# Last pair's new sample state among its value projections, one norm chain for prompt and sample, and a shared tile for accumulators and gates

## The chip, the cores and the metric

The kernel runs on one core of one Trainium2 chip. The metric is the device time of one execution in microseconds, the median of several runs; lower is better. A profiled execution gives the trace that is quoted here. Its engines are TensorE (PE, with PEld for the weight loads), VectorE (DVE), ScalarE (ACT), GpSimd (POOL) and SyncE (SP), which issues most DMAs.

## The reference

One step of a hybrid decoder layer, for a prompt of 1024 tokens and a sample of 8 sequences with 4 new tokens each (32 rows). An RMSNorm feeds one input projection. Head group A is sparse attention: an indexer scores the keys, the top 256 are chosen, and 8 query heads attend to them, with a position bias. For the sample the keys lie in a paged cache of 8192 positions. Head group B is retention with 8 heads of 64. Both branches are gated, concatenated and projected, then comes a post-norm, the residual and a gated embedding. What matters here is group B:

```python
def step(S, inp):                       # chunks of 128 tokens
    inter = einsum('bchk,bhkv->bchv', qc * dec_in, S)
    scores = einsum('bchk,bshk->bhcs', qc, kc) * dmat
    intra = einsum('bhcs,bshv->bchv', scores, vc)
    S = S * dec_chunk + einsum('bchk,bchv->bhkv', kc * dec_out, vc)
    return S, inter + intra
...
yb = silu(gb) * _head_norm(ob)          # mean and variance of each head's 64 values
```

It is done for the prompt (state from zero, eight chunks) and for the sample (state given for each sequence, one chunk of 4). The final states of both are outputs.

## The kernel before, in words

The program is written in one order, and a scheduler decides the order in which each engine gets it, from a model of the times; the engines then run their own queues in that order and wait on semaphores. The buffers of a pool are reused tile by tile: who takes a buffer over waits for the last use of the old tile, its DMAs included.

After the indexer and the prompt's selection, retention runs over four pairs of heads (hp = 0 to 3; here pair 0 to pair 3). Each pair has two stages on TensorE:

- the query/key stage: eight blocks of 128 tokens, 24 matmuls each (L276 to L278, tile pqk; three products of split fp32 values), and eight matmuls for the sample (L285). Each block is rotated on VectorE (L1047 to L1049) and GpSimd (L1051, L1052).
- the value stage: the same for values and gates (tile pvg). take_vg copies each block's values (L1060, vv) and takes silu of its gates (L1062, sg) on ScalarE. Then come the chunk's matmuls: two transposes (L1068, L1069), scores (L1078), masked on VectorE (L1079, sm), the state's update (L1489, added up in sbd at L1494) and the outputs (L1498, L1500), which ScalarE copies into the accumulator (L1502, acc, one tile of 9 blocks, the ninth for the sample).

After block 7 the sample's turn (ret_sample, from L1129): its old states are loaded (s0), its values and gates taken (vvs, sgs), its outputs computed (L1139, L1141) and added up (L1143 to L1145), and its new state is made: a masked copy of the values for each head (vm, L1150), one matmul for each (dst, L1152), added to the old state (sso, L1156, L1157) and written out (L1158).

Then norm_gate, twice. For the prompt, 16 columns (8 blocks by 2 heads): statistics (L1088, L1089), variance plus epsilon (gv, L1094), square root on ScalarE and reciprocal (gy, L1097, L1098), one Newton step (gz, L1104 to L1106, L1112, L1113), the scaling of each column (three of four on ScalarE, L1117; the fourth on VectorE, L1119), the multiplication with the gates (L1122; on GpSimd, and on VectorE for pair 3), and one DMA to a buffer in DRAM (yb_d, L1123). For the sample the same with two columns of 32 rows.

Beside these run pieces of two generators: the bisection that finds the sample's 256th score (during pairs 0 and 1, at high priority, L872 to L1017, with a conditional part behind a branch at L976 through which all engines go), and the sample's selection (from pair 1 on, L1203 to L1282, with L1234, and gathers of key and value rows, L1170). Matmuls of both stand between those of the pairs.

PSUM banks: three for pqk and pvg (tag b), three for ret and dst (tag c). acc has one buffer; sg has ten, vv three. All these tiles are in the pool rt on the right side of SBUF. When retention ends, rt is closed, and attention's tiles take the same addresses: the first score tiles (L) lay over norm_gate's temporaries and over acc, vv, sg, qkT and sm.

Attention begins with the bias tiles (near, L1583, from a DMA of toep, L1551), the scores on TensorE (sa, L1596, L1597), the score with bias and maximum on VectorE (L1602), the exponential on ScalarE (L1605).

Of the kernel before, what the change touches and what calls it, by code (L numbers as in the profile page):

```python
# [10 lines left out]
F32 = mybir.dt.float32  # L11
# [4 lines left out]
AF = mybir.ActivationFunctionType  # L16
# [6 lines left out]
NS = 32  # L23
# [97 lines left out]
def tile_step(ctx: ExitStack, tc: tile.TileContext, I, O):  # L121
# [911 lines left out]
    s0 = rt.tile([128, 8, 128], F32, name="s0")  # L1033
    for t in (*sbd, s0):
        nc.gpsimd.memset(t, 0.0)
# [19 lines left out]
    def take_vg(src, rows, tb, hp, name):  # L1055

        vv = rt.tile([128, 2, 64], F32, tag="vv", bufs=3, name=f"vv{name}")
        sg = rt.tile([128, 128], F32, tag="sg", bufs=10, name=f"sg{name}")
        for j in range(2):
            nc.scalar.activation(vv[:rows, j, :], src[:rows, j * 64:j * 64 + 64], AF.Copy,  # L1060
                                 scale=vsc[:rows, tb, 2 * hp + j:2 * hp + j + 1])
        nc.scalar.activation(sg[:rows], src[:rows, 128:256], AF.Silu)  # L1062
        return vv.rearrange("p h v -> p (h v)"), sg
# [18 lines left out]
    def norm_gate(acc, sgs, ntb, rows, tb0, hp):  # L1082

        nh = ntb * 2
        st = rt.tile([128, 16, 6], F32, tag="st", bufs=2, name="bst")
        mv = rt.tile([128, 16, 2], F32, tag="mv", bufs=2, name="bmv")
        for i in range(nh):
            nc.vector.bn_stats(st[:rows, i, :], acc[:rows, i // 2, (i % 2) * 64:(i % 2) * 64 + 64])  # L1088
            nc.vector.bn_aggr(mv[:rows, i, :], st[:rows, i, :])  # L1089
        v = rt.tile([128, 16], F32, tag="gv", bufs=1, name="gv")  # L1090
        y = rt.tile([128, 16], F32, tag="gy", bufs=1, name="gy")
        z = rt.tile([128, 16], F32, tag="gz", bufs=1, name="gz")
        v_, y_, z_ = v[:rows, :nh], y[:rows, :nh], z[:rows, :nh]
        nc.vector.tensor_tensor(v_.rearrange("p (t h) -> p t h", h=2),  # L1094
                                mv[:rows, :nh, 1].rearrange("p (t h) -> p t h", h=2),
                                epsn[:rows, tb0:tb0 + ntb, 2 * hp:2 * hp + 2], op=ALU.add)
        nc.scalar.activation(y_, v_, AF.Sqrt)  # L1097
        nc.vector.reciprocal(y_, y_)  # L1098
        one = [slice(i, i + 1) for i in range(nh)]
        if nh == 2:  # L1100
            for i in one:
                nc.vector.tensor_scalar(z_[:, i], y_[:, i], y_[:, i], v_[:, i], op0=ALU.mult, op1=ALU.mult)
        else:
            nc.vector.tensor_tensor(z_, y_, y_, op=ALU.mult)  # L1104
            nc.vector.tensor_tensor(z_, z_, v_, op=ALU.mult)
        nc.vector.tensor_scalar(z_, z_, -0.5, 1.5, op0=ALU.mult, op1=ALU.add)  # L1106
        if nh == 2:
            for n, i in enumerate(one):
                nc.vector.tensor_scalar(y_[:, i], y_[:, i], z_[:, i], None, op0=ALU.mult)
                nc.vector.tensor_scalar(z_[:, i], mv[:rows, n, 0:1], y_[:, i], -1.0, op0=ALU.mult, op1=ALU.mult)  # L1110
        else:
            nc.vector.tensor_tensor(y_, y_, z_, op=ALU.mult)  # L1112
            nc.vector.scalar_tensor_tensor(z_, mv[:rows, :nh, 0], -1.0, y_, op0=ALU.mult, op1=ALU.mult)  # L1113
        for i in range(nh):
            a = acc[:rows, i // 2, (i % 2) * 64:(i % 2) * 64 + 64]
            if i % 4 < 3:
                nc.scalar.activation(a, a, AF.Identity, bias=z_[:, i:i + 1], scale=y_[:, i:i + 1])  # L1117
            else:
                nc.vector.tensor_scalar(a, a, mv[:rows, i, 0:1], y_[:, i:i + 1],  # L1119
                                        op0=ALU.subtract, op1=ALU.mult)  # L1120
        for t in range(ntb):
            (nc.vector if hp == 3 else nc.gpsimd).tensor_tensor(acc[:rows, t, :], acc[:rows, t, :], sgs[t][:rows], op=ALU.mult)  # L1122
        nc.sync.dma_start(yb_d[:rows, tb0:tb0 + ntb, hp, :], acc[:rows, :ntb, :])  # L1123
# [5 lines left out]
    def ret_sample(hp, qk, sh, acc):  # L1129
# [3 lines left out]
        vv, sg = take_vg(sh, NS, 8, hp, f"s{hp}")  # L1133
        r, qkT, sm = chunk_mm(qk, vv, 8, NS, smask, hp)
        qm = rt.tile([128, 8, NS], F32, tag="vm", bufs=1, name="qm")
# [8 lines left out]
        for j in (0, 2, 3):  # L1144
            nc.vector.tensor_tensor(acc[:NS, 8, :], r[NS * j:NS * j + NS, 0:128], acc[:NS, 8, :], op=ALU.add)  # L1145
        d = bank("dst", "c")
# [13 lines left out]
        return sg  # L1160
# [289 lines left out]
    for hp in range(4):  # L1450
# [22 lines left out]
        acc = rt.tile([128, 9, 128], F32, tag="acc", bufs=1, name=f"acc{hp}")  # L1473
        sgs = []
# [3 lines left out]
        for tb in range(8):  # L1478
# [5 lines left out]
            vv, sg = take_vg(pt, 128, tb, hp, f"{hp}_{tb}")  # L1484
            sgs.append(sg)
# [16 lines left out]
            nc.scalar.copy(acc[:, tb, :], o)  # L1502
            if tb == 7:
                sgS = ret_sample(hp, qks[8], sh, acc)
        steps(hp)
        so = rt.tile([128, 64], F32, tag="so", bufs=2, name=f"so{hp}")
# [4 lines left out]
        norm_gate(acc, sgs, 8, 128, 0, hp)  # L1511
        norm_gate(acc[:, 8:9, :], [sgS], 1, NS, 8, hp)
# [335 lines left out]
```

## Time and profile before

| | us |
|---|---|
| median of 3 runs (lowest, highest) | 1051.2 (1048.44, 1052.79) |
| profiled execution, its own time | 1050.72 |
| its span | 1048.9 |
| TensorE busy | 991.8 |
| pair 1's value stage begins | 432.3 |
| pair 2 begins | 470.0 |
| pair 3 begins | 503.8 + 40.6 = 544.4 |
| pair 3's value projections end | 623.0 |
| first attention score on VectorE | 647.2 |

The mean granted clock of TensorE is 0.976 of full speed. The page of the profile gives busy time by engine and the chain of work that ended last; views of the trace give stretches by stage (windows), waits by engine, groups of instructions by line, and the instructions one by one (timeline). In rows "out<-in" names the tiles, "<-DVE mn" what ended a wait.

### The profile page before, as it was taken

The numbers are of one execution on the slowest core, as the hardware profiler recorded it, in microseconds if no ns is written. First come the engines' busy times: TensorE is split into PE (matmuls) and PEld (weight loads), VectorE is DVE, ScalarE is ACT, GpSimd is POOL, SyncE is SP. The second block draws the span as 40 slices with busy tenths as digits, with TensorE's granted clock in tenths as the row PEclk, the third lists the DMA queues.
The fourth block names the chain that finished last, engine by engine and source line by source line (L and its number), as shares of the span: only waits on it lengthen the run. The fifth ranks groups of instructions, "written<-read, shape, count | busy, mean of one in ns | idle before, by whom it ended". The sixth has DMA issues, their size and how long they took to land.

```text
span 1048.9 us, 19845 instructions
## 1 busy us (share of the span) xinstructions
PE 991.8 (95%) x7375; PEld 838.2 (80%) x7375; DVE 681.4 (65%) x2022; ACT 503.1 (48%) x1090; POOL 320.8 (31%) x425
## 2 busy tenths in 40 slices
PE   4999998999999899999899995999999999999998
PEld 3999997766776898889788783666666999999998
DVE  6847668898492657969949937787763423873332
ACT  5545565885434487612342335656545523442211
POOL 4203223121301522705803512634330522332200
PEclk9999999999999999999899995999999999999999
DMA  8211235545443311311210724533211312432211
GB/s 291 71 61 51 96 97 190 186 148 177 130 161 115 76 33 43 81 45 47 64 54 21 190 65 128 162 78 109 73 56 48 118 42 81 148 116 87 83 41 38
DMA packets 98310, 102.25 MB, mean 97 GB/s; under 512 B 21346, under 2 KB 88386, under 8 KB 95906
## 3 DMA queue, kind: packets, MB, share of 16 engines
q1 hardware_dynamic: 92450, 74.74, 23.7%
q0 software_dynamic: 5760, 26.22, 8.0%
q8 instruction: 58, 0.95, 0.4%
q14 instruction: 42, 0.34, 0.1%
HBM read 79.25 MB, written 21.68 MB: 96 GB/s over the span
## 4 chain that ended last, share of the span: by engine, by line
PE 45%; DVE 6%; DMA 2%; issue 1%; POOL 1%; ACT 1%; SPq 0%; DVEq 0%; ACTq 0%; POOLq 0%
PE ob L1620 4%; PE ptp L1612 4%; PE pg L276 3%; PE pg L278 3%; PE pg L277 3%; PE po L276 3%; PE po L277 3%; PE po L278 2%; PE sa L1596 2%; PE pvg L276 2%; PE pvg L277 2%; PE pvg L278 2%; PE sa L1597 1%; PE pty L1667 1%; PE pqk L276 1%
## 5 line engine op out<-in xcount | busy, mean ns | idle before, releaser
L1170 POOL DMA_INDIRECT kvs<-in_cache_kv,idx x64 | 64.2, 1003 | 84.1 <-ACT pT L1617 49.1
L276 PE MATMUL pvg<-whi_vgb,xh 128*128 128x256 f32 x256 | 76.2, 298 | 3.0 <-ACT sg L1062 1.8
L276 PE MATMUL pqk<-whi_qkb,xh 128*128 128x256 f32 x256 | 75.0, 293 | 3.3 <-DVE rp L1049 3.3
L277 PE MATMUL pvg<-wlo_vgb,xh 128*128 128x256 f32 x256 | 75.6, 295 | 0.0
L278 PE MATMUL pvg<-whi_vgb,xl 128*128 128x256 f32 x256 | 75.1, 293 | 0.0
L277 PE MATMUL pqk<-wlo_qkb,xh 128*128 128x256 f32 x256 | 74.1, 290 | 0.0
L276 PE MATMUL po<-whi_o,yTh 128*128 128x256 f32 x256 | 73.1, 286 | 0.4 <-DVE yaT L1631 0.4
L278 PE MATMUL pqk<-whi_qkb,xl 128*128 128x256 f32 x256 | 73.2, 286 | 0.0
L278 PE MATMUL po<-whi_o,yTl 128*128 128x256 f32 x256 | 72.8, 285 | 0.0
L276 PE MATMUL pg<-whi_g,yTh 128*128 128x256 f32 x256 | 72.7, 284 | 0.0
L277 PE MATMUL po<-wlo_o,yTh 128*128 128x256 f32 x256 | 72.7, 284 | 0.0
L278 PE MATMUL pg<-whi_g,yTl 128*128 128x256 f32 x256 | 72.3, 283 | 0.0
L277 PE MATMUL pg<-wlo_g,yTh 128*128 128x256 f32 x256 | 72.2, 282 | 0.0
L1605 ACT ACTIVATE L<-L,mn 128x128 f32<-128x128 f32 (+7 forms) x64 | 49.6, 777 | 15.0 <-DVE mn L1602 14.6
L511 DVE SCALAR_TENSOR_TENSOR score<-r,wi,score 128x384 f32<-128x384 f32 (+5 forms) x42 | 41.0, 976 | 23.0 <-ACT r L507 21.7
L1805 DVE TENSOR_TENSOR sgm<-pu,sgm 128x256 f32<-128x256 f32 x32 | 13.6, 424 | 64.8 <-PE pu L278 61.1
L276 PEld LDWEIGHTS pvg<-whi_vgb,xh 128*128 128x128 f32 x256 | 49.8, 195 | 5.4 <-ACT sg L1062 2.2
L276 PEld LDWEIGHTS pqk<-whi_qkb,xh 128*128 128x128 f32 x256 | 49.0, 191 | 6.4 <-issue 5.5
L186 POOL TENSOR_TENSOR wlo_g<-wraw_g,whi_g 128x256 fp32r<-128x256 f32 x32 | 27.1, 881 | 87.8 <-ACT whi_g L185 87.7
L1051 POOL TENSOR_TENSOR qk<-rp,rp 128x128 f32<-128x128 f32 (+1 forms) x36 | 29.6, 821 | 78.7 <-DVE rp L1048 49.3
L507 ACT ACTIVATE r<-si 128x384 f32<-128x384 f32 (+5 forms) x48 | 36.3, 758 | 32.0 <-PE si L365 30.6
L278 PEld LDWEIGHTS pqk<-whi_qkb,xl 128*128 128x128 f32 x256 | 49.1, 192 | 2.4 <-issue 2.4
(545 smaller groups left out, 3317.9 us busy)
## 6 DMA issues: line engine op xcount, KB each, us to landing
wraw_qkb<-in_w_in SPq DMA_DIRECT2D x16, 256.0 KB, 4.1
wraw_vgb<-in_w_in SPq DMA_DIRECT2D x16, 256.0 KB, 3.8
wraw_o<-in_w_out SPq DMA_DIRECT2D x8, 512.0 KB, 5.6
qas<-qas_d SPq DMA_DIRECT2D x8, 512.0 KB, 5.1
xr<-in_x_prompt SPq DMA_DIRECT2D x8, 512.0 KB, 3.9
wraw_g<-in_w_ple_gate SPq DMA_DIRECT2D x8, 512.0 KB, 4.3
out_y_prompt<-sgm SPq DMA_DIRECT2D x32, 128.0 KB, 1.7
qas_d<-qst SPq DMA_DIRECT2D x8, 384.0 KB, 2.7
```

The costliest lines, as they stand in the source:

```text
L186: nc.gpsimd.tensor_tensor(lo[:, k, :n], raw, hi[:, k, :n].bitcast(F32), op=ALU.subtract)
L276: nc.tensor.matmul(pt[:, :n], ah, hi[:, k, :n], start=(k == 0), stop=False)
L277: nc.tensor.matmul(pt[:, :n], ah, lo[:, k, :n], start=False, stop=False)
L278: nc.tensor.matmul(pt[:, :n], al, hi[:, k, :n], start=False, stop=(k == kc - 1))
L507: nc.scalar.activation(r[:, :n], s[:, :n], AF.Relu)
L511: nc.vector.scalar_tensor_tensor(sc, r[:, :n], wi[:, qb, h:h + 1], sc, op0=ALU.mult, op1=ALU.add)
L1051: nc.gpsimd.tensor_tensor(q4[:, :, 0, :], t1[:rows, :, 0, :], t2[:rows, :, 0, :], op=ALU.subtract)
L1170: return nc.gpsimd.indirect_dma_start(out=dst, out_offset=None, in_=kvflat, in_offset=bass.IndirectOffsetOnAxis(ap=idx, axis=0))
L1596: nc.tensor.matmul(s[:, :wc], qas[:, h, :], kah[kv][:, c:c + wc], start=True, stop=False)
L1605: behind[0] = nc.scalar.activation(L[:, :n], L[:, :n], AF.Exp, bias=least, scale=-1.0, accum_out=sm[:, i4:i4 + 1])
L1612: nc.tensor.transpose(tp[:, i4 * 128:i4 * 128 + 128], P[i4][:, kb * 128:kb * 128 + 128], ident)
L1620: nc.tensor.matmul(ob[64 * o:64 * o + 64, :256], vtok[:, kb, kv * 64:kv * 64 + 64], pT[:, o * 256:o * 256 + 256], start=(kb == 0), stop=(k ...
```

## The change

Five things, in one diff:

- A tile ag of 9 blocks by 2 by 128 values holds accumulators (index 0) and gates (index 1). It replaces acc (one buffer) and sg (ten buffers), and has one buffer.
- norm_gate treats prompt and sample in one chain of 18 columns; the rows of the sample's two columns above 32 hold 1.0. The tiles gv, gy, gz, mv and st have one buffer. Two DMAs write yb_d, one for the prompt, one for the sample.
- ret_sample is split: sample_in (old states, values and gates), ret_sample (outputs) and new_state (vm, dst, sso). For pair 3, sample_in and new_state stand after block 3; for the others new_state stands after norm_gate.
- The sample's values have a tile of their own (vvs).
- The tiles of eight tags, ag and the norm's among them, are allocated first in rt, at the low addresses (120672 to 133344). The first score tiles of attention (151264 to 167648) no longer lie over them; the second and third group's key/value tiles (115936 to 134368) now do.

The lines move: before's L1062, L1117, L1502, L1152, L1596, L1602 are L1070, L1115, L1504, L1157, L1603, L1609 after it.

```diff
+    first = {t: rt.tile(shape, F32, name=t, tag=t, bufs=n) for t, shape, n in (
+        ("vm", [128, 8, NS], 1), ("mv", [128, 18, 2], 1), ("gv", [128, 18], 1), ("gy", [128, 18], 1),
+        ("gz", [128, 18], 1), ("st", [128, 18, 6], 1), ("ag", [128, 9, 2, 128], 1), ("so", [128, 64], 2))}
+
+    def rtile(shape, tag, n, name):
+        if tag in first:
+            return first.pop(tag)
+        return rt.tile(shape, F32, tag=tag, bufs=n, name=name)
...
-    def take_vg(src, rows, tb, hp, name):
-
-        vv = rt.tile([128, 2, 64], F32, tag="vv", bufs=3, name=f"vv{name}")
-        sg = rt.tile([128, 128], F32, tag="sg", bufs=10, name=f"sg{name}")
+    def take_vg(src, rows, tb, hp, name, sg, tag="vv"):
+
+        vv = rt.tile([128, 2, 64], F32, tag=tag, bufs=3 if tag == "vv" else 1, name=f"vv{name}")
...
+    mv = first.pop("mv")
+    nc.gpsimd.memset(mv[:, 16:, :], 1.0)
...
+    def norm_gate(ag, hp):
+
+        acc = ag[:, :, 0, :]
+        st = rtile([128, 18, 6], "st", 1, "bst")
+        rows = [128] * 16 + [NS] * 2
+        for i, n in enumerate(rows):
+            nc.vector.bn_stats(st[:n, i, :], acc[:n, i // 2, (i % 2) * 64:(i % 2) * 64 + 64])
+            nc.vector.bn_aggr(mv[:n, i, :], st[:n, i, :])
+        v, y, z = (rtile([128, 18], t, 1, t) for t in ("gv", "gy", "gz"))
+        nc.vector.tensor_tensor(v.rearrange("p (t h) -> p t h", h=2),
+                                mv[:, :, 1].rearrange("p (t h) -> p t h", h=2),
+                                epsn[:, :, 2 * hp:2 * hp + 2], op=ALU.add)
+        nc.scalar.activation(y, v, AF.Sqrt)
+        nc.vector.reciprocal(y, y)
+        nc.vector.tensor_tensor(z, y, y, op=ALU.mult)
+        nc.vector.tensor_tensor(z, z, v, op=ALU.mult)
+        nc.vector.tensor_scalar(z, z, -0.5, 1.5, op0=ALU.mult, op1=ALU.add)
+        nc.vector.tensor_tensor(y, y, z, op=ALU.mult)
+        nc.vector.scalar_tensor_tensor(z, mv[:, :, 0], -1.0, y, op0=ALU.mult, op1=ALU.mult)
+        for i, n in enumerate(rows):
+            a = acc[:n, i // 2, (i % 2) * 64:(i % 2) * 64 + 64]
             if i % 4 < 3:
-                nc.scalar.activation(a, a, AF.Identity, bias=z_[:, i:i + 1], scale=y_[:, i:i + 1])
+                nc.scalar.activation(a, a, AF.Identity, bias=z[:n, i:i + 1], scale=y[:n, i:i + 1])
             else:
-                nc.vector.tensor_scalar(a, a, mv[:rows, i, 0:1], y_[:, i:i + 1],
-                                        op0=ALU.subtract, op1=ALU.mult)
-        for t in range(ntb):
-            (nc.vector if hp == 3 else nc.gpsimd).tensor_tensor(acc[:rows, t, :], acc[:rows, t, :], sgs[t][:rows], op=ALU.mult)
-        nc.sync.dma_start(yb_d[:rows, tb0:tb0 + ntb, hp, :], acc[:rows, :ntb, :])
+                nc.vector.tensor_scalar(a, a, mv[:n, i, 0:1], y[:n, i:i + 1], op0=ALU.subtract, op1=ALU.mult)
+        for t in range(9):
+            n = rows[2 * t]
+            (nc.vector if hp == 3 else nc.gpsimd).tensor_tensor(acc[:n, t, :], acc[:n, t, :], ag[:n, t, 1, :], op=ALU.mult)
+        nc.sync.dma_start(yb_d[:, :8, hp, :], acc[:, :8, :])
+        nc.sync.dma_start(yb_d[:NS, 8, hp, :], acc[:NS, 8, :])
...
-    def ret_sample(hp, qk, sh, acc):
+    def sample_in(hp, sh, ag):
         for j in range(2):
             js = slice(j * 64, j * 64 + 64)
             nc.sync.dma_start(s0[js, :, js], I["state_ret"][0, :, 2 * hp + j].rearrange("b d v -> d b v"))
-        vv, sg = take_vg(sh, NS, 8, hp, f"s{hp}")
+        return take_vg(sh, NS, 8, hp, f"s{hp}", ag[:, 8, 1, :], "vvs")
+
+    def ret_sample(hp, qk, vv, ag):
+        acc = ag[:, :, 0, :]
         r, qkT, sm = chunk_mm(qk, vv, 8, NS, smask, hp)
-        qm = rt.tile([128, 8, NS], F32, tag="vm", bufs=1, name="qm")
+        qm = rtile([128, 8, NS], "vm", 1, "qm")
...
+    def new_state(hp, qk, vv):
...
-        acc = rt.tile([128, 9, 128], F32, tag="acc", bufs=1, name=f"acc{hp}")
-        sgs = []
+        ag = rtile([128, 9, 2, 128], "ag", 1, f"ag{hp}")
...
-            vv, sg = take_vg(pt, 128, tb, hp, f"{hp}_{tb}")
-            sgs.append(sg)
+            vv = take_vg(pt, 128, tb, hp, f"{hp}_{tb}", ag[:, tb, 1, :])
...
-            nc.scalar.copy(acc[:, tb, :], o)
+            nc.scalar.copy(ag[:, tb, 0, :], o)
+            if tb == (3 if hp == 3 else 7):
+                vvs = sample_in(hp, sh, ag)
+                if hp == 3:
+                    new_state(hp, qks[8], vvs)
             if tb == 7:
-                sgS = ret_sample(hp, qks[8], sh, acc)
+                ret_sample(hp, qks[8], vvs, ag)
...
-        norm_gate(acc, sgs, 8, 128, 0, hp)
-        norm_gate(acc[:, 8:9, :], [sgS], 1, NS, 8, hp)
+        norm_gate(ag, hp)
+        if hp < 3:
+            new_state(hp, qks[8], vvs)
```

More of the change, by code (lines that the diff above doesn't have):

```diff
@@ L1062, in take_vg @@
         nc.scalar.activation(sg[:rows], src[:rows, 128:256], AF.Silu)
-        return vv.rearrange("p h v -> p (h v)"), sg
+        return vv.rearrange("p h v -> p (h v)")
     def chunk_mm(qk, vv, tb, rows, mask_ap, hp):
@@ L1080, in chunk_mm @@
         return r, qkT, sm
[L1082 to L1115, printed above, removed]
@@ L1159, in ret_sample @@
             O["ret_state_sample"][0, :, 2 * hp:2 * hp + 2].rearrange("b h d v -> (h d) b v"), so)
-        return sg
     sel_d = dram.tile([2, NS * 64], BF16, name="sel_d")
@@ L1501, in tile_step @@
                                  start=(tb == 0 and j == 0), stop=(j == 1))
-            nc.scalar.copy(acc[:, tb, :], o)
+            nc.scalar.copy(ag[:, tb, 0, :], o)
[3 more added lines that the diff above has]
+                    new_state(hp, qks[8], vvs)
             if tb == 7:
-                sgS = ret_sample(hp, qks[8], sh, acc)
+                ret_sample(hp, qks[8], vvs, ag)
         steps(hp)
-        so = rt.tile([128, 64], F32, tag="so", bufs=2, name=f"so{hp}")
+        so = rtile([128, 64], "so", 2, f"so{hp}")
         for j in range(2):
```

## The prediction

> **What bounds the kernel now.** I read the page first: the totals, then the chain that ended last.
>
> ```profile
> span 1048.9 us, 19845 instructions
> PE 991.8 (95%) x7375; PEld 838.2 (80%) x7375; DVE 681.4 (65%) x2022; ACT 503.1 (48%) x1090; POOL 320.8 (31%) x425
> PE 45%; DVE 6%; DMA 2%; issue 1%; POOL 1%; ACT 1%; SPq 0%; DVEq 0%; ACTq 0%; POOLq 0%
> ```
>
> TensorE is busy for 991.8 of 1048.9 us. Time can come only from the 57 us in which it idles, from stretches at a low granted clock, or from matmuls moved. So I next asked for busy time by stage. The rows are: pair 1's value and gate projections, pair 2's query/key stage, its value stage, the same two of pair 3, and the passage into attention. Columns: busy time and count for PE, PEld, DVE, ACT, POOL, then clock, DMA share and GB/s.
>
> ```profile
> 432.30:470.00 37.70, 35.22 (x290) 32.05 (x288) 27.84 (x92) 11.81 (x37) 14.09 (x26) 1.00 0.27 68
> 470.00:503.80 33.80, 33.80 (x284) 29.69 (x284) 30.76 (x81) 7.41 (x19) 19.84 (x20) 1.00 0.19 58
> 503.80:544.40 40.60, 36.63 (x275) 33.31 (x275) 28.15 (x83) 19.64 (x52) 17.95 (x25) 0.92 0.22 55
> 544.40:584.20 39.80, 39.10 (x342) 33.35 (x341) 35.63 (x138) 9.12 (x27) 13.21 (x22) 1.00 0.15 42
> 584.20:623.00 38.80, 37.11 (x309) 34.34 (x308) 23.68 (x102) 14.45 (x49) 12.16 (x21) 0.96 0.48 123
> 623.00:647.20 24.20, 12.22 (x76) 6.97 (x74) 15.80 (x69) 12.02 (x33) 5.70 (x8) 0.65 0.54 160
> ```
>
> The passage (last row) is the worst stretch: 12 of 24.2 us idle, at a clock of 0.65. The four rows before it hold 0 + 3.97 + 0.70 + 1.69 = 6.4 us of idle time. Their clock costs (1 - 0.92) x 36.6 = 2.9 and (1 - 0.96) x 37.1 = 1.5 us more. The waits of TensorE name the two largest single causes: first for 470 to 623, then for the passage.
>
> ```profile
> PE pfx L1234 <- DVE sm L1232: 2.6, 1, 2.6
> ...
> PE sa L1596 <- DVE mn L1602: 8.1, 1, 8.1
> ```
>
> The first is a step of the sample's top-k selection, late on VectorE. The second is the first attention score, late because VectorE is still normalising pair 3. The timeline of the passage, in order of start (start, duration):
>
> ```profile
> 630.18 1.62 DVE L1583 TENSOR_TENSOR near<-toep,cst 128x512 f32<-128x512 f32 x2 [0.71 <-DMA toep<-toep_d]
> 632.28 0.35 DVE L1088 BATCH_NORM_STATS2 bst<-acc 128x6 f32<-128x64 f32 x2
> 633.27 1.97 PE L1152 MATMUL dst<-vm,qk 32*64 32x512 f32 x2 [1.99 <-DVE vm L1150]
> 633.81 0.15 DVE L1094 TENSOR_TENSOR gv<-bmv,cst 128x16 f32<-128x16 f32 x1
> 638.00 1.41 DVE L1156 TENSOR_TENSOR sso<-dst,s 64x512 f32<-64x512 f32 x2 [1.63 <-PE dst L1152]
> 639.44 0.17 DVE L1106 TENSOR_SCALAR gz<-gz 128x16 f32<-128x16 f32 x1
> 640.39 4.09 ACT L1117 ACTIVATE acc<-acc,gz,gy 128x64 f32<-128x64 f32 x12 [6.18 <-DVE gz L1113]
> 646.89 0.28 DVE L1122 TENSOR_TENSOR acc<-acc,sgs 32x128 f32<-32x128 f32 x1 [0.72 <-ACT acc L1117]
> 647.20 0.29 DVE L1602 CUSTOM_DVE_ANT_0 L<-sa,near 128x128 f32<-128x128 f32 x1
> ...
> 647.41 0.28 DVE L1602 CUSTOM_DVE_ANT_0 L<-sa,near 128x128 f32<-128x128 f32 x1
> ```
>
> VectorE is in program order: L1106 stands behind L1156, which waits for the half-speed dst matmuls. Then come the identities, the gates, and a whole second chain for the sample, up to 647.20.
>
> **Part 1, the passage: a gain of 6.1 us, of which 2.1 are paid elsewhere.** On TensorE, before, after the sample's last retention matmuls (L1139, L1141; dst is the new state, sa the first scores):
>
> ```order
> L1139 MATMUL ret_7771<-s0_3680,qm_7781 32x128 x8
> L1141 MATMUL ret_7771<-vvs3_7766,sm_7776 32x64 x2
> L1152 MATMUL dst_7797<-vm_7798,qk3_8_7368 64x512
> L1152 MATMUL dst_7797<-vm_7801,qk3_8_7368 64x512
> L1596 MATMUL sa_7962<-kahi_7908,qas0_7942 128x128
> L1597 MATMUL sa_7962<-kalo_7909,qas0_7942 128x128
> ```
>
> And now, at the same place:
>
> ```order
> L1500 MATMUL ret_7684<-sbd1_3679,qkT_7687 128x128
> L1502 MATMUL ret_7684<-vv3_7_7680,sm_7689 128x64 x2
> L1141 MATMUL ret_7701<-s0_3680,qm_7711 32x128 x8
> L1143 MATMUL ret_7701<-vvs3_7501,sm_7706 32x64 x2
> L1603 MATMUL sa_7864<-kahi_7810,qas0_7844 128x128
> L1604 MATMUL sa_7864<-kalo_7811,qas0_7844 128x128
> ```
>
> The dst matmuls are gone from here; they now stand among pair 3's value projections. In VectorE's program the first score still stands behind the whole norm, its eight gates and the sample's gate. So the passage gets shorter, but it does not vanish. With T for the end of the value projections (623.0): the bias tiles (near) end at 631.8, so T+8.8, set by a DMA that is not touched. From the first stats behind them (632.28) to gv (633.81) before took 1.5 us with a 0.7 us tile of the new state in between; with the sample's two columns and three adds put in, I take 2.1: T+10.9. Square root, reciprocal and five short steps at 0.17 each, with two handovers between engines: about 2.1, T+13.0. Fourteen identities at 4.09/12 = 0.34: 4.8, T+17.8. The last gates: 0.3, T+18.1. Before it was 647.2 - 623.0 = 24.2. The gain is 6.1 us. The moved dst matmuls cost their time in the stream; all sixteen, by line:
>
> ```profile
> L1152 PE MATMUL dst<-vm,qk x16: 587/638/1112, 423.5 to 636.9; 32*64 32x512 f32 x16
> ```
>
> Four a pair, at 587 to 638 ns: 2.1 us overlapped. Net -4.1. Bounds: -6.5, if they hide in gaps, to -2, if the clock or the bias DMA is later. The wait for the first score stays some 8 us long, so the low clock there stays too.
>
> **Part 2, a new wait between pairs 0 and 1: +16 us.** Gates and accumulators now share one tile (ag), of which there is one. Before, the gate of pair 1's first block (L1062) had a buffer of its own. Now its silu must wait until pair 0's ag has been normalised, gated and written out by both DMAs. ScalarE before (pair 1's blocks; sg1_0 is the first gate):
>
> ```order
> L1117 ACTIVATE acc0_4193<-acc0_4193,gz_4961,gy_4960 128x64 x12
> L1097 ACTIVATE gy_5002<-gv_5001 32x2
> L185 CAST whi_qkb2_5461<-wraw_qkb20_5463 128x1024
> L1060 ACTIVATE vv1_0_5517<-pvg_5471,cst_63 128x64 x2
> L1062 ACT_TABLE_LOAD
> L1062 ACTIVATE sg1_0_5518<-pvg_5471 128x128
> ```
>
> Now (ag_3687 is pair 0's tile, ag1_5423 pair 1's):
>
> ```order
> L976 UNCONDITIONAL_BRANCH
> L1068 ACTIVATE vv1_2_5631<-pvg_5584,cst_63 128x64 x2
> L1115 ACTIVATE ag_3687<-ag_3687,gz_3685,gy_3684 128x64 x12
> L1115 ACTIVATE ag_3687<-ag_3687,gz_3685,gy_3684 32x64 x2
> L1070 ACT_TABLE_LOAD
> L1070 ACTIVATE ag1_5423<-pvg_5448 128x128
> ```
>
> Pair 0's identities have moved behind the third block's values and behind the branch (L976). On VectorE, the rows around that branch are now:
>
> ```order
> L976 UNCONDITIONAL_BRANCH x2
> L992 SCALAR_TENSOR_TENSOR ssm_3791<-ssm_3791 128x1
> L1109 TENSOR_SCALAR gz_3685<-gz_3685 128x18
> L994 CAST sbits_3787<-ssm_3791 128x1
> L1087 TENSOR_TENSOR sm_5640<-ret_5635,cst_63 128x128
> L1110 TENSOR_TENSOR gy_3684<-gy_3684,gz_3685 128x18
> L996 TENSOR_TENSOR sbits_3787<-sbits_3787 128x1
> L1496 TENSOR_TENSOR sbd0_3678<-ret_5566,sbd1_3679 64x64 x2
> L1111 SCALAR_TENSOR_TENSOR gz_3685<-mv_3682,gy_3684 128x18
> L872 TENSOR_SCALAR sjk_3780,ssm_3791<-Xt_3778,sbits_3787 128x2080
> L1117 TENSOR_SCALAR ag_3687<-ag_3687,mv_3682,gy_3684 128x64 x4
> ```
>
> Pair 0's norm is split: its end has slid past the branch of the bisection and past L872. The times of these in the trace of before: the gates' group on GpSimd and its sample gate, the write's landing (pair 0's, then all pairs'), the first gate, the fourth block's first matmul, the first accumulator copy, the end of the branch, L872 and the wait on it.
>
> ```profile
> L1122 POOL TENSOR_TENSOR acc<-acc,sg 128x128 f32<-128x128 f32 x8 | 5.5, 713 | 0.0
> L1122 POOL TENSOR_TENSOR acc<-acc,sgs 32x128 f32<-32x128 f32 x1 | 1.4, 1431 | 0.0
> ...
> DMA to landing us min/median/max: 4.5/4.5/4.5
> ...
> DMA to landing us min/median/max: 1.4/3.1/9.2
> ...
> 440.63 0.28 ACT L1062 ACTIVATE sg<-pvg 128x128 f32<-128x128 f32 x1
> ...
> 445.95 0.37 PE L276 MATMUL pvg<-whi_vgb,xh 128*128 128x256 f32 x1
> ...
> 450.19 0.27 ACT L1502 COPY acc<-ret 128x128 f32<-128x128 f32 x1 [4.34 <-PE ret L1500]
> ...
> 452.96 0.22 DVE L992 SCALAR_TENSOR_TENSOR ssm<-ssm 128x1 f32<-128x1 f32 x1 [3.13 <-DVEq L976]
> 453.60 2.38 DVE L872 TENSOR_SCALAR_CACHE_REDUCE sjk<-Xt,sbits 128x2080 bf16<-128x2080 f32 x1
> ...
> 456.04 0.38 PE L874 MATMUL stot<-ssm,groupr 128*128 128x1 f32 x2 [1.49 <-DVE sjk L872]
> ```
>
> The branch ends at 452.96 as before (bounds 451.5 and 455.5: the same bisection stands ahead of it, between other steps). L1111 follows 1.8 us later, at 454.8. Fourteen identities take it to 459.6; VectorE's four columns come after L872, at about 458.3. GpSimd's nine gates at 0.5 to 0.7, the last longer, end at about 462 (460 to 465). The write took 4.5 here and 3.1 in the median of all; I take 3: 465. The silu, held with its table load, adds about 1, and the fourth block, whose projection needs the PSUM bank, starts at 466 instead of 445.95. By then TensorE has done about 6.4 us of what stood behind 445.95 before (the chunk matmuls of three blocks, the small ones of the bisection, the 1.49 us wait). Of the 470.0 - 445.95 = 24 us to pair 2, 17.7 remain: 483.7. A clock loss comes on top; rows around two earlier gaps:
>
> ```profile
> 592.00:597.00 5.00, 4.68 (x25) 4.55 (x26) 4.91 (x24) 2.53 (x6) 2.91 (x7) 0.66 0.99 264
> ...
> 517.00:525.00 8.00, 5.98 (x27) 5.54 (x28) 7.78 (x30) 4.67 (x16) 5.47 (x11) 0.57 0.01 2
> ```
>
> They lost 0.34 x 5 = 1.7 and 0.43 x 8 = 3.4 us of clock; I take 2.3, so pair 2 begins at 486, +16. Bounds: with the early values of each step +11, with the late ones +21.
>
> Two rules of the Trainium skill speak here. "TensorE: Matmul & The Clock Gate", section on why this matters for your kernels, warns of idle gaps of TensorE over about 3 us, and Part 1 puts the return to full speed at about 3.4 us of sustained work: a loss of 1.7 us. The first row agrees, the second is double; by the rule the sum would be 0.6 us less. "SBUF — State Buffer", section on the DMA setup-cost knee, gives 2 us plus bytes over 436 GB/s: an estimate of 3.2 us for the 512 KB write. The measured 4.5 is longer; by the row the sum would be 1.3 us more.
>
> **Part 3, what is paid back: -10.** While TensorE stands still, VectorE and GpSimd go on with the selection, so pairs 2 and 3 find it further ahead. At most the 6.4 + 2.9 + 1.5 = 10.8 us of the four rows above go; I take 10 (bounds 4 and 10.8, since waits on rope and on pair 2's own state are not selection).
>
> **Part 4, new cost in pairs 2 and 3: +3.** In VectorE's program the selection groups (L1271, L1277, L1282) move from pair 3's query/key stage into pair 2's value stage, where VectorE now also has all of pair 1's leftovers.
>
> ```profile
> L1271 DVE TENSOR_SCALAR oh<-slot,sm 128x256 bf16<-128x256 bf16 x32 | 13.3, 445 | 2.0 <-PE psl L1273 2.0
> L1277 DVE TENSOR_TENSOR le<-psl,cst 128x384 bf16<-128x384 f32 (+1 forms) x11 | 5.9, 537 | 0.1
> L1282 DVE TENSOR_REDUCE row<-le 128x6 f32<-128x384 bf16 (+1 forms) x11 | 5.8, 525 | 0.0
> ```
>
> Together 25 us, most of which ran in the row from 544.4 (VectorE busy for 35.6). Pair 2's value stage has 40.6 us, of which VectorE filled 28.2; with over half of these groups added it is near full, so I take single waits of 3 us; bounds 0 and 7. The same shared tile makes pair 2's and 3's first gates wait for the write too, but the norm runs early there and the blocks' banks cover most of it.
>
> **The sum.** -4.1 + 16 - 10 + 3 = +4.9 on the profiled execution of 1050.7 us (span 1048.9 and 1.8 around it), which lies 0.5 us under the median of 1051.2: 1050.7 + 4.9 is 1055.6, I say 1055.5. The rest is taken to be the same: fewer short steps on VectorE, and the new addresses of the score tiles, cost or give nothing I can find, since before, the second score (647.41) follows the first (647.20) without a wait.
>
> **The rivals.** *A. The stall is short (faster).* If pair 0's norm runs ahead of the branch in fact, or the gates and the write are quick (write 1.4, as its shortest in other pairs), the fourth block starts near 457 and the stall is +7. Paid back in full, with 1 of new cost: -4.1 + 7 - 10.8 + 1 = -7: 1044. Against it: the order of VectorE is fixed, and the norm's end stands behind the branch. *B. Little is paid back (slower).* If VectorE stays the late one in pairs 2 and 3 with the moved groups, -4.1 + 16 - 4 + 6 = +14: 1065. It decides if VectorE's busy time in pair 2's value stage passes about 95%. For it: 35.6 of 39.8 us in pair 3's query/key stage already. *C. No effect.* A stall at its low end, 12, against full payback: -4.1 + 12 - 10.8 + 3 = 0: 1051. *D. Part 1 does nothing*, because the first score waits for the bias or for key tiles: +4 on the forecast, 1059.5; it lies in the range.
>
> **How the numbers follow.** The bound for a difference is 0.5%, about 5.3 us, what a measurement of this kernel can tell from no change: under 1046 is faster, over 1056.5 slower. The forecast case with its own spread (1049 to 1062, D in it) has 0.55: 0.25 of it no change and 0.30 slower, as 1055.5 lies near the edge. A has 0.22 (faster), B 0.10 (slower), C 0.13 (no change). That gives 0.22, 0.38 and 0.40. The range of eight in ten reaches from A's value to B's: 1044 to 1065.
>
> **What would show it.** In the profile after: TensorE idle by 12 to 18 us in pair 1's value stage, ended by ScalarE's L1070, which waits for the write of ag; query/key of pair 2 some 16 us later; the wait on L1234 gone; the passage 18 us instead of 24, with no dst in it. The forecast is wrong if that idle time is under 8 us, or if pair 3's value projections end less than 3 or more than 16 us later than at 623.0.

## The result, and the profile after

The changed kernel takes 1060.2 us (median of 6 runs, 1057.24 to 1062.48) against 1050.1 (6 runs, 1048.44 to 1052.79): a ratio of 1.0088, 95% interval 1.0061 to 1.0115. It is slower by 0.9%. The forecast was 1055.5, with 0.40 on slower and a range of 1044 to 1065: right in its direction and its range, 4.7 us too low.

The profiled execution took 1060.73 us. The page of the profile, totals and chain, as shown of before:

```profile
span 1059.0 us, 19805 instructions
PE 990.1 (93%) x7375; PEld 841.2 (79%) x7375; DVE 669.5 (63%) x1986; ACT 499.9 (47%) x1084; POOL 313.5 (30%) x426
PE 48%; DVE 4%; DMA 2%; ACT 2%; issue 1%; POOL 0%; another core or an unknown queue 0%; SPq 0%; ACTq 0%; DVEq 0%; POOLq 0%
```

The same 7375 matmuls, and VectorE, ScalarE and GpSimd a little less busy. TensorE is busy for 1.7 us less, so the 10 us are idle time: 68.9 us instead of 57.1. The stages, in the order of the table of before (pair 1's value stage, pair 2, pair 2's value stage, pair 3, its value stage, the passage):

```profile
433.00:483.20 50.20, 41.02 (x289) 36.46 (x288) 36.74 (x112) 17.97 (x54) 14.75 (x26) 0.83 0.25 68
483.20:518.70 35.50, 35.37 (x294) 30.48 (x294) 34.12 (x100) 11.19 (x28) 17.03 (x24) 1.00 0.14 35
518.70:560.90 42.20, 38.88 (x331) 36.17 (x330) 23.07 (x102) 14.96 (x48) 13.68 (x23) 0.92 0.22 60
560.90:594.80 33.90, 33.90 (x297) 29.83 (x297) 28.95 (x116) 11.04 (x28) 19.23 (x34) 1.00 0.28 77
594.80:631.10 36.30, 36.30 (x295) 32.21 (x294) 14.60 (x58) 10.76 (x38) 3.22 (x7) 1.00 0.41 102
631.10:649.70 18.60, 7.71 (x70) 6.12 (x68) 12.45 (x55) 11.47 (x30) 5.70 (x8) 0.70 0.59 172
```

Pair 2 begins 13.2 us later than before (483.2 against 470.0). The value projections of pair 3 end only 8.1 later, so 5.1 are won back on the way. The passage shrinks from 24.2 to 18.6 us, and the first score stands at 649.7, 2.5 later than before. Up to here the sum is what was forecast, and better by 2.4 us. The rest comes behind the first score, in a stage that the diff doesn't touch. Attention, from the first score to the output projection, cut into 13, 20, 20, the middle and the last 20 us. Before:

```profile
647.20:660.20 13.00, 12.32 (x66) 9.39 (x67) 9.36 (x37) 8.23 (x28) 7.62 (x7) 0.60 0.40 116
660.20:680.20 20.00, 18.46 (x137) 11.49 (x135) 15.41 (x64) 13.40 (x39) 12.08 (x13) 1.00 0.64 192
680.20:700.20 20.00, 20.00 (x156) 12.87 (x155) 15.77 (x59) 11.52 (x28) 8.74 (x8) 1.00 0.36 93
700.20:793.20 93.00, 93.00 (x692) 59.13 (x691) 66.85 (x239) 55.03 (x109) 34.95 (x37) 1.00 0.26 74
793.20:813.20 20.00, 19.59 (x181) 12.24 (x178) 6.06 (x17) 8.24 (x18) 0.54 (x2) 1.00 0.11 37
```

After:

```profile
649.70:662.70 13.00, 12.58 (x69) 9.42 (x69) 9.88 (x41) 8.33 (x29) 7.49 (x7) 0.64 0.50 142
662.70:682.70 20.00, 15.74 (x111) 9.92 (x111) 12.40 (x51) 11.19 (x33) 10.28 (x12) 0.91 0.52 154
682.70:702.70 20.00, 19.41 (x136) 11.28 (x132) 15.10 (x59) 10.71 (x27) 9.74 (x9) 1.00 0.41 122
702.70:803.70 101.00, 101.00 (x748) 64.57 (x745) 70.09 (x249) 57.64 (x117) 38.59 (x39) 1.00 0.26 76
803.70:823.70 20.00, 17.79 (x169) 11.26 (x166) 5.48 (x15) 7.64 (x16) 0.00 (x0) 1.00 0.04 13
```

The stretch is 166.0 us before and 174.0 after, for the same 1222 matmuls (one that spans a cut is counted in two rows). Idle time is 2.6 before and 7.5 after. Three places stand out: the second row (4.26 idle, clock 0.91), the third (0.59), and the last (2.21 against 0.41).

Why should attention change at all? The order of each engine's queue is set by the scheduler's model of the times, and in attention it differs. Counted in the two traces, from the first score to the output projection, 682 of TensorE's 1222 matmuls stand at another place of its queue, the first of them 11 us behind the first score, and 181 of VectorE's 412 instructions. The last products of the sample show it best. In the changed kernel the sample's last sums (oS) come behind the prompt's last (ob), before they did not; the first and the last start stand behind the durations in each row. The rows by tile, ob and oS, of before:

```profile
L1620 PE MATMUL ob<-pT,vtok x288: 378/380/689, 653.6 to 812.2; 128*64 128x256 f32 x144
...
L1397 PE MATMUL oS<-kvs,PT x128: 272/273/297, 691.8 to 811.7; 128*32 128x128 f32 x128
```

And of after:

```profile
L1627 PE MATMUL ob<-pT,vtok x288: 379/379/690, 655.5 to 818.0; 128*64 128x256 f32 x144
...
L1401 PE MATMUL oS<-kvs,PT x128: 272/273/297, 701.3 to 822.4; 128*32 128x128 f32 x128
```

So at the end there is nothing left to fill the sample's last chain with, and TensorE waits for VectorE's copy of the weights for the sample's new tokens (PN), a wait that before does not have:

```profile
PE oS L1396 <- DVE PN L1393: 1.5, 1, 1.5
```

### The profile page after: what moved, and what is told of

It is laid out like the page before. It is cut to its first block, busy times and chain, and to the rows that moved or that the text cites. A ratio compares the mean times of both kernels' runs of the same rounds, so it can differ in the third digit from the quotient of the medians.

```text
span 1059.0 us, 19805 instructions
## 1 busy us (share of the span) xinstructions
PE 990.1 (93%) x7375; PEld 841.2 (79%) x7375; DVE 669.5 (63%) x1986; ACT 499.9 (47%) x1084; POOL 313.5 (30%) x426
## 4 chain that ended last, share of the span: by engine, by line
PE 48%; DVE 4%; DMA 2%; ACT 2%; issue 1%; POOL 0%; another core or an unknown queue 0%; SPq 0%; ACTq 0%; DVEq 0%; POOLq 0%
PE ob L1627 4%; PE ptp L1619 4%; PE pg L276 3%; PE pg L278 3%; PE pg L277 3%; PE po L276 3%; PE po L277 3%; PE po L278 3%; PE pvg L276 2%; PE sa L1603 2%; PE pvg L277 2%; PE pvg L278 2%; PE sa L1604 2%; PE pqk L278 1%; PE pqk L276 1%; PE pqk L277 1%
## 5 line engine op out<-in xcount | busy, mean ns | idle before, releaser
L1603 PE MATMUL sa<-kahi,qas 128*128 128x512 f32 (+3 forms) x96 | 41.1, 430 | 12.3 <-DVE mn L1609 12.3
L277 PEld LDWEIGHTS pvg<-wlo_vgb,xh 128*128 128x128 f32 x256 | 50.6, 198 | 1.3 <-issue 0.8
```

Source lines behind the costliest of these rows:

```text
L277: nc.tensor.matmul(pt[:, :n], ah, lo[:, k, :n], start=False, stop=False)
L1603: nc.tensor.matmul(s[:, :wc], qas[:, h, :], kah[kv][:, c:c + wc], start=True, stop=False)
```

## The experiments

Two theories for the 8 us behind the first score: the **order** (the scheduler's new order of attention costs them, whatever brought it about) and the **addresses** (later key and value tiles now lie over the tiles allocated first, and attention waits for them). For retention: the **write** (pair 1's gates wait for the shared tile to be written out) and the **place** (the norm's end behind the branch is enough). All ratios are to the kernel before on the same chip.

### Gates in buffers of their own

```diff
-        ("gz", [128, 18], 1), ("st", [128, 18, 6], 1), ("ag", [128, 9, 2, 128], 1), ("so", [128, 64], 2))}
+        ("gz", [128, 18], 1), ("st", [128, 18, 6], 1), ("ag", [128, 9, 128], 1), ("so", [128, 64], 1))}
...
+        sg = rt.tile([128, 128], F32, tag="sg", bufs=10, name=f"sg{name}")
```

> The changed kernel, but with the gates in ten buffers of their own again and only the accumulators in the shared tile (one buffer of the small output tile so gives the room). If the wait of pair 1's first gates for the write of pair 0's tile makes the stall, the stall of 13 us in pair 1's value stage shrinks to about 7 (the gates still stand behind pair 0's fourteen identities on ScalarE, and those behind the branch), the 3.3 us wait in pair 2 goes, and the time is about 1060 - 8 = 1052. If the place of the norm behind the branch alone makes it, the stall stays at 12 or more and the time at 1058 to 1060. Attention is in the order of the changed kernel here, so both theories on attention expect the 7.6 us behind the first score to stay.

Pair 1's value stage, then pair 2's first stage:

```profile
429.10:473.70 44.60, 40.20 (x287) 35.51 (x286) 28.71 (x92) 17.85 (x52) 14.95 (x27) 0.89 0.29 76
473.70:511.20 37.50, 34.72 (x292) 30.36 (x291) 35.97 (x98) 6.88 (x18) 19.41 (x21) 1.00 0.13 32
```

The stage takes 44.6 us, against 50.2 in the changed kernel and 37.7 before: 7 us of stall are left of 12.5, as the theory of the write expected, and the wait of 3.3 us for pair 2's first gate is gone. That the norm's place makes the other half is argued, not shown: with this edit the scheduler also orders retention anew. Attention stands in the order of the changed kernel. The time is 1059.8 (1051.5 to 1061.5), ratio 1.0075 (1.0049 to 1.0102): nearly that of the changed kernel. The profiled execution was the fastest of the six, so its trace is not typical of the others, and where they lose their time isn't shown. The time expected, 1052, was missed: less stall, hardly less time.

### The early new state alone

```diff
+            if tb == (3 if hp == 3 else 7):
+                vvs, sgS = sample_in(hp, sh)
+                if hp == 3:
+                    new_state(hp, qks[8], vvs)
             if tb == 7:
-                sgS = ret_sample(hp, qks[8], sh, acc)
+                ret_sample(hp, qks[8], vvs, acc)
+                if hp < 3:
+                    new_state(hp, qks[8], vvs)
```

> The kernel before, with only the last pair's new state (and its sample values, in a tile of their own) moved behind its fourth block; two norm chains, gates and addresses as before (one buffer fewer of so and st). The first score comes some 4 us earlier against the end of the projections, the projections end about 2 us later: first score near 645. The scheduler puts attention in nearly the order of the changed kernel. If that order costs the 7.6 us behind the first score, the time is near 1050 - 2 + 7.6 = 1056. If the new addresses cost them, they are absent here, and it is near 1048.

1059.1 us, ratio 1.0078 (1.0050 to 1.0106). The passage takes 19.9 us (628.6 to 648.5), 4.3 less than before, as expected; but the projections end 5.6 later, not 2, so the first score comes 3.5 us later than the 645 expected. Pair 2 already begins at 474.7, 4.7 later than before: pair 1's value stage takes 43.7 us, with 3.8 of idle time, of which a wait for a gate (L1062) makes 2.3. Why that gate is late isn't shown. From the first score to the output projection it is 172.2 us. The time lies 3 us over the theory of the order (1056) and 11 over that of the addresses (1048).

### One chain alone

```diff
-        norm_gate(acc, sgs, 8, 128, 0, hp)
-        norm_gate(acc[:, 8:9, :], [sgS], 1, NS, 8, hp)
+        norm_gate(acc, sgs + [sgS], hp)
```

> The kernel before, with only the norm as one chain of 18 columns. Its pair 0 norm stands ahead of the branch, so no stall in pair 1's value stage is expected (pair 2 begins within 2 us of 470). The passage loses the sample's own chain, about 2.4 us, and waits for the sample's sums instead: first score 1 to 3 us earlier. Attention is in nearly the order of the changed kernel: by the theory of the order 1050 - 2 + 7.6 = 1056, by the theory of the addresses near 1048.

1055.4 us, ratio 1.0047 (1.0020 to 1.0074). Pair 2 begins at 468.4, so no stall; the first score comes at 644.7, 2.5 earlier than before. From there to the output projection it is 173.7 us instead of 166.0. What is gained is lost behind the first score.

### The addresses alone

```diff
+    first = {t: rt.tile(shape, F32, name=t, tag=t, bufs=n) for t, shape, n in (
+        ("vm", [128, 8, NS], 1), ("mv", [128, 16, 2], 2), ("gv", [128, 16], 1), ("gy", [128, 16], 1),
+        ("gz", [128, 16], 1), ("st", [128, 16, 6], 2), ("acc", [128, 9, 128], 1), ("so", [128, 64], 2))}
```

> The kernel before, with only the addresses changed: the accumulators, the norm's tiles, the state's tiles and so are allocated first; gates, chains and every engine's order are as before. By the theory of the addresses (later key and value tiles wait for tiles that lie under them) attention loses several us: 1055 to 1058. By the theory of the order nothing changes: within 0.3% of 1050.

1051.4 us, ratio 1.0005 (0.9986 to 1.0024): no change. Every engine's order is the same, and the new places of the score tiles bring neither loss nor gain. The tiles allocated first are smaller here than in the changed kernel (acc instead of ag); the next run has that kernel's addresses exactly, and it too speaks against the theory of the addresses.

### The changed kernel with attention in the old order

A few steps that multiply the last pair's scale by 1.0 shift the scheduler's model by fractions of a microsecond; with eight of them it lays attention exactly as before, while retention stays as in the changed kernel. The trace bears that out: up to the first score only the eight steps differ from the changed kernel, and from there to the output projection TensorE, VectorE and GpSimd run in the order of before.

```diff
+        for _ in range(8 if hp == 3 else 0):
+            nc.vector.tensor_scalar(y, y, 1.0, None, op0=ALU.mult)
         nc.vector.scalar_tensor_tensor(z, mv[:, :, 0], -1.0, y, op0=ALU.mult, op1=ALU.mult)
```

> The changed kernel with eight more small steps in the last pair's norm (its scale times 1.0, about 1 us in all on VectorE). Retention stands in the order of the changed kernel, but with these eight steps the scheduler puts attention in exactly the order of the kernel before. If the order of attention costs the 7.6 us behind the first score, the stretch from first score to output projection falls from 174 back to about 166 us and the time to about 1060 + 1 - 7 = 1054. If it is retention's end that makes attention slow (a shorter passage, other buffers, other gathers), the time is about 1061.

1051.9 us, ratio 1.0030 (1.0005 to 1.0054). Its interval lies below that of the changed kernel (1.0061 to 1.0115). The eight steps, in the timeline:

```profile
640.96 1.65 DVE L1112 TENSOR_SCALAR gy<-gy 128x18 f32<-128x18 f32 x8
```

The stage of the stall, and the stretch from first score to output projection:

```profile
431.90:480.60 48.70, 39.98 (x288) 35.41 (x286) 36.41 (x112) 17.96 (x54) 14.88 (x26) 0.86 0.25 70
...
648.00:812.70 164.70, 162.30 (x1222) 104.18 (x1222) 113.38 (x412) 96.06 (x218) 63.47 (x65) 0.98 0.32 93
```

The last products, ob and oS:

```profile
L1629 PE MATMUL ob<-pT,vtok x288: 379/379/689, 653.8 to 811.7; 128*64 128x256 f32 x144
...
L1403 PE MATMUL oS<-kvs,PT x128: 272/273/297, 691.3 to 811.3; 128*32 128x128 f32 x128
```

The stall is there (48.7 us), and attention takes 164.7 us. The kernel has 1.65 us more work in its passage and is still 0.58 percentage points faster than the changed one. This is the order, shown by itself.

### The kernel before with attention in the new order

```diff
+            for _ in range(6 if hp == 3 else 0):
+                nc.vector.tensor_scalar(y_, y_, 1.0, None, op0=ALU.mult)
             nc.vector.scalar_tensor_tensor(z_, mv[:rows, :nh, 0], -1.0, y_, op0=ALU.mult, op1=ALU.mult)
```

> The kernel before with six such small steps in the last pair's prompt norm (about 0.7 us). Retention stands in the order of before, but attention in exactly the order of the changed kernel. Theory of the order: first score to output projection rises from 166 to 172 or 174 us, time about 1051 + 1 + 6 = 1058. Otherwise: about 1052.

1055.0 us, ratio 1.0063 (1.0041 to 1.0084), where six steps by themselves are worth 6 x 1.65/8 = 1.2 us. Up to the first score only the six steps differ from before, and attention stands in the order of the changed kernel. The stretch of attention, in an execution that was the slowest of the twelve (1059.6):

```profile
649.70:820.00 170.30, 165.53 (x1223) 106.40 (x1223) 113.12 (x413) 95.35 (x218) 65.61 (x65) 0.96 0.29 87
```

The wait at its end:

```profile
PE oS L1394 <- DVE PN L1391: 1.5, 1, 1.5
```

And the last ob and oS:

```profile
L1622 PE MATMUL ob<-pT,vtok x288: 379/379/690, 656.1 to 812.6; 128*64 128x256 f32 x144
...
L1399 PE MATMUL oS<-kvs,PT x128: 272/273/418, 695.9 to 818.5; 128*32 128x128 f32 x128
```

Six small steps make the kernel before 0.6% slower, most of it by the new order: the sample's sums run 6 us past the prompt's, and the wait on PN is there again. Stretch and time lie some 2 and 3 us under what was expected (172 to 174, and 1058).

### One chain, and gates apart, in the old order

Steps of the same form as above, ten in the kernel with one chain and eight in that with gates apart, were meant to put attention back. In the second they do, but for one exchange of two VectorE steps, and up to the first score only the eight steps are new. In the first they do not.

> The kernel before with the norm as one chain, and ten small steps in the last pair's (about 1 us), with which attention stands in exactly the order of before. Theory of the order: the run with one chain alone took 1055.4; this one takes 1055.4 + 1 - 6 = 1050. Otherwise: about 1056.5.

1048.2 us, ratio 1.0014 (0.9991 to 1.0037), against 1.0047 without the ten steps, which are worth about 2 us, 0.2%, themselves. The intervals overlap. And attention does not stand in the order of before here, other than expected: counted in the traces, 466 of TensorE's 1222 matmuls of attention stand at another place, the first 13 us behind the first score. It is a third order, neither before's nor the changed kernel's, and attention takes 164.7 us in it. What one chain is worth in the order of before isn't shown.

> The changed kernel with gates in ten buffers of their own and eight small steps (about 1 us), with which attention stands in exactly the order of before. The run with gates apart took 1059.8 in the median, but 1051.5 in its profiled execution. Theory of the order: 1059.8 + 1 - 7 = 1054. Otherwise: about 1060.

1049.7 us, ratio 1.0025 (1.0002 to 1.0049), against 1.0075 (1.0049 to 1.0102): a third exchange of the order under the same retention, worth half a percent again. With the shared tile it was 1.0030, so with the order held fixed the shared tile costs nothing that these runs can tell.

### Two attempts at a faster kernel

Gates apart, one chain, new addresses, and for the last pair the gates on GpSimd and half of the identities on VectorE; once with the early new state, once without (four and three small steps keep the old order).

```diff
-            if i % 4 < 3:
+            if i % 4 < (2 if hp == 3 else 3):
...
-            (nc.vector if hp == 3 else nc.gpsimd).tensor_tensor(
+            nc.gpsimd.tensor_tensor(
```

> A version meant to keep the gain of the passage without the two costs: one chain, the last pair's new state early, the new addresses, gates in buffers of their own, and for the last pair the gates on GpSimd and half instead of three quarters of the identities on ScalarE; four small steps keep attention exactly in the order of before. In the passage ScalarE's identities end about 1.5 us sooner and no gate stands ahead of the first score: 14 to 15 us from the end of the projections against 24.2 before. Pair 1's value stage still has a stall of about 7 us (gates behind the norm that stands across the branch), of which 5 are won back in pairs 2 and 3, and the dst matmuls cost 2: first score near 642 to 645, time 0.3 to 0.6% under that of before run beside it. If what the passage gains is lost again behind the first score (ScalarE's exponentials as the bound there), the time is that of before within 0.2%.

> The same without the early new state: the last pair's new state stays in the passage, where its matmuls and VectorE steps delay the norm. First score 19 to 21 us behind the projections; no 2 us in the stream. If the early new state is worth 2 us net, this is 0.2% slower than the version with it; if the passage's gain is lost behind the first score, both take the time of before.

1052.6 us, ratio 1.0045 (1.0023 to 1.0067), and 1052.8, ratio 1.0036 (1.0015 to 1.0056): both slower than before, where a gain of 0.3 to 0.6% or none was expected; what the early new state is worth can't be told from the two. Of the first, TensorE's wait for the last chunk's state, the square root, and the steps ahead of the first score:

```profile
637.54 0.80 PE L1503 MATMUL ret<-sbd,qkT 128*128 128x128 f32 x2 [2.64 <-DVE sbd L1499]
...
642.62 0.22 ACT L1105 ACTIVATE gy<-gv 128x18 f32<-128x18 f32 x1 [0.54 <-DVE gv L1102]
...
644.95 2.58 DVE L1119 TENSOR_SCALAR ag<-ag,mv,gy 128x64 f32<-128x64 f32 x8
...
647.57 0.29 DVE L1612 CUSTOM_DVE_ANT_0 L<-sa,near 128x128 f32<-128x128 f32 x1
```

The passage takes 19.2 us here, not 15: the square root comes 14.3 us behind the projections (628.3) instead of 11.9 in the changed kernel (642.97 - 631.1, below), since TensorE waits 2.6 us ahead of the sample's sums, and VectorE's eight scalings (2.58 us) took the place of the gates. The other takes 21.1, at the end of what was expected. Pairs 1 and 2 lose 5 us, and this time it isn't won back (628.3 and 627.5 at the end of the projections). No version beat the kernel before.

## Why the prediction was right or wrong

**The passage (Part 1)** was right: 18.6 us against 18.1, a gain of 5.6 instead of 6.1. (Its net is -4.0, not -4.1: 6.1 less 2.1.) The bias tiles, the square root and the first score, behind the last gate; ScalarE's fourteen identities between the last two took 4.8, as summed:

```profile
639.53 1.29 DVE L1590 TENSOR_TENSOR near<-toep,cst 128x512 f32<-128x512 f32 x2 [1.09 <-DMA toep<-toep_d]
...
642.97 0.22 ACT L1105 ACTIVATE gy<-gv 128x18 f32<-128x18 f32 x1 [2.72 <-DVE gv L1102]
...
649.68 0.29 DVE L1609 CUSTOM_DVE_ANT_0 L<-sa,near 128x128 f32<-128x128 f32 x1
```

The profiles of two experiments split it: early new state 4.3, one chain 1.5, together 5.8. The 2.1 us taken for the moved dst matmuls were not measured by themselves.

**The stall (Part 2)** came where it was forecast and by the forecast steps, 13.2 us instead of 16 and within its bounds. The steps, in order of start:

```profile
450.86 0.22 DVE L992 SCALAR_TENSOR_TENSOR ssm<-ssm 128x1 f32<-128x1 f32 x1 [3.09 <-DVEq L976]
...
452.06 0.18 DVE L1111 SCALAR_TENSOR_TENSOR gz<-mv,gy 128x18 f32<-128x18 f32 x1
452.27 4.75 ACT L1115 ACTIVATE ag<-ag,gz,gy 128x64 f32<-128x64 f32 x14 [2.85 <-DVE gz L1111]
454.84 2.92 POOL L1120 TENSOR_TENSOR ag<-ag 128x128 f32<-128x128 f32 x7 [0.27 <-DVE ag L1117]
457.39 0.37 SPq L1121 DMA_DIRECT2D yb_d<-ag  x1
460.89 1.28 ACT L1070 ACT_TABLE_LOAD   x1 [3.88 <-DVE sjk L1016]
```

And what TensorE waited for in that stage, the two longest:

```profile
PE ret L1500 <- DVE sbd L1496: 4.1, 2, 2.8
PE pvg L276 <- ACT ag L1070: 1.7, 1, 1.7
```

So the sign that was named, 12 to 18 us of idle time ended by L1070, did not show in that form. The stage has 9.2 us of idle time (2.5 before), and L1070 ends 1.7 of them: steps that wait for VectorE stand ahead of the fourth block in TensorE's queue. The rest of the 12.5 us by which the stage is longer is matmuls that take longer, 41.0 us instead of 35.2 for as many.

The branch ended 2.1 us earlier than I took, and GpSimd's gates kept pace with ScalarE (done 457.8, not 462). ScalarE's table load then waits 3.9 us. The trace names a VectorE step, which ends at 460.8, but by the program the load waits for the two writes as well. They were issued at 457.4 and 457.9 and, by the trace's records of their semaphores, landed at 460.6 and 460.8: 3.2 us for the large one, against 4.5 measured before and 3 taken. By the Trainium skill, page "SBUF — State Buffer", section on the DMA setup-cost knee, a write of 512 KB would take 3.2 us, an estimate; this execution agrees, the one before did not. (Against the 3 taken, the row's 4.5 would have made the sum 1.5 us more, not 1.3.)

The fourth block starts at 462.5, not 466. What its clock costs can be read from two stretches, the block and what follows it:

```profile
462.50:467.90 5.40, 5.38 (x25) 5.38 (x26) 2.79 (x13) 0.95 (x6) 0.85 (x3) 0.50 0.71 225
467.90:470.90 3.00, 3.00 (x27) 3.00 (x26) 3.00 (x2) 0.95 (x4) 0.97 (x1) 1.00 0.00 0
```

At a granted clock of 0.50 a matmul begins every 0.21 us, at 1.00 every 0.12: over the block's 24, 2.3 us, the clock loss that was taken.

**What is paid back and new (Parts 3 and 4)** was right in its sum, and that is in part luck. From +13.2 to +8.1 with 2.1 for the moved dst matmuls is -7.2; forecast -10 + 3. The payback came: the wait on L1234 is gone, and pair 3's two stages are without an idle microsecond. Part 4's cost came from elsewhere. It took VectorE to be near full in pair 2's value stage, with the moved selection; VectorE is busy for 23.1 of 42.2 us there, less than before. The new wait, 3.3 us (the idle time of the row from 518.7), is that of pair 2's first gate for the write of pair 1's tile, which Part 4 named and took to be mostly covered. So the sum of Parts 1 to 4, +4.9, measured +2.5 at the first score. With the order held, the whole change is +0.30% (0.05 to 0.54), 3.1 us, of which the eight steps are 1.65. What is left for the change itself, about 1.5 us, can't be told from nothing.

**What failed** is the last step of the sum: "The rest is taken to be the same". I looked at the rest for addresses and step counts and not at its order. The rows of attention differ in order. Measured, the new order is worth 0.6% of the kernel (1.0088 against 1.0030; 1.0063 with before's retention), as much as all the rest of the change together and more. Rival *B* (little is paid back, 1065) lies as near to the measured time as the forecast, but its mechanism did not happen: the payback came, and VectorE's share in pair 2's value stage, on which it hung, was 55%, not 95%. That the measured time still lies in the forecast range is luck: the range was wide on account of *B*, and the cost that filled it was in none of its terms.

**What is settled and what is open.** In the new order, or one that differs from it by a few rows, the stretch took 174.0, 170.3, 172.2, 173.7 and 170.3 us in five profiles; in the old 166.0, 170.3, 164.7, 167.0, 166.1 and 168.6 in six: 172.1 against 167.1 in the mean, and the two groups touch at 170.3. Each is a single execution. Two losses are in all five and in none of the six: 1.8 us of idle time in the last 20 us (the wait on PN and what is around it), and 0.5 between 33 and 53 us behind the first score. They make 2.3 of the 5.0 us. The other 2.7 lie in the first 33 us and in longer matmul time and differ from run to run (idle 1.2 to 4.3 us in the second slice); which of the reordered rows brings them about isn't shown.

## What to carry to other kernels

Where a scheduler sets the order from modelled times, a change in one stage can reorder every stage behind it, so compare the order to the end of the program before you call the rest the same, and hold the order fixed (here by a few idle steps) before you judge the edit. Check in the trace that it is held: of five kernels meant to have the old order, one had a third. A timing that moves by half a percent after an edit may be the lottery of the order: the kernel before lost 0.6% to six multiplications by 1.0. And a buffer that is shared between the first work of a stage and the last of the one before it makes the later stage wait for as long as that last work is late, even where, as here, it is won back so far that the total doesn't tell.

## What the runs showed that was not expected

In three of the twelve profiles, of either order, ScalarE stops for 3.1 to 4.4 us and VectorE for 0.9 to 2.0, 21 to 22 us behind the first score, and are released together by something that the trace doesn't name. In the kernel with only the addresses changed:

```profile
666.61 0.29 DVE L1611 CUSTOM_DVE_ANT_0 L<-sa,mask 128x128 f32<-128x128 f32 x1 [2.01 <-remote]
666.64 0.59 ACT L1626 COPY pT<-ptp 128x512 f32<-128x512 f32 x1 [4.35 <-remote]
667.28 1.12 PE L1629 MATMUL ob<-pT,vtok 128*64 128x256 f32 x4 [3.04 <-ACT pT L1626]
```

TensorE loses 3.0 us there and then about 1.5 us of clock (0.91 over the 16.9 us in which it is busy in that slice), about the 4.3 us by which this profile's attention is longer than that of before in the same order. The changed kernel's profile has it too (3.2 us on ScalarE at 670.9), so a part of its 8 us is this and not the order; the ratios of many runs are the firmer measure. What it is stays open.
